# Accumulating transfers of a column pair's eight blocks into the HBM copy of x, written one per following row pair, in a two-layer retention and latent-attention trunk

## The chip, the cores and the metric

The kernel runs on one core of a Trainium2 chip. The metric is the device time of one execution in microseconds. Before the change three executions took 2494.59, 2503.17 and 2501.63 us; the median is 2501.63 us. One further execution was recorded by the profiler.

## The reference

The program is a trunk of two layers over 256 tokens (two row tiles of 128) with a residual stream `x` of width 2048, all in float32. Layer 0 is a RetNet retention layer with eight heads and a squared-ReLU MLP; layer 1 is a multi-head latent attention layer (MLA) with sixteen heads and the same MLP. What the change touches is how `x` takes in the result of a block:

```python
x = x + retention(h, ret_w_in[layer], ret_w_out[layer], ret_cos, ret_sin)
...
x = x + sq_relu_mlp(rms_norm(x, norm_mlp[layer]), mlp_w1[layer], mlp_w2[layer])

def sq_relu_mlp(h, w1, w2):
    return jnp.square(jax.nn.relu(h @ w1)) @ w2
```

`w1` is 2048 x 8192 and `w2` 8192 x 2048, so nearly all the work is matrix products whose weights come from HBM once.

## The kernel before, in words

**Products.** A float32 operand is split into a high part (a cast on ScalarE, line 183) and a low part (a subtraction on VectorE, line 184), and each product is made of three matmuls (lines 359 to 361). `quad` (line 285) works on one chunk of weights: 1 MB, 128 x 2048 numbers, loaded by the SP queue (line 288) into one of three `raw` buffers. A chunk holds a pair of weight rows (256 rows) for a pair of 512-wide output columns, as four 512-wide blocks. It is multiplied either plainly, with eight products (24 matmuls), or in a seven-product form after Winograd (21 matmuls), which needs extra sums of the weights on VectorE (lines 318 to 323). This document calls the work of one chunk a row, or row pair.

**Column pairs.** `gemm_pair` (line 336) runs 8 rows (4 groups of 2048 hidden columns give the MLP's second product 8 rows each) into PSUM blocks c11, c12, c21, c22, p1, p5, p6 and p7. `kinds` says which rows have seven products; for the first column pair of an MLP group these are rows 3, 5 and 7. `pair_out` (line 371) then copies c22, c12, c11, c21, p1 and p5 to SBUF on ScalarE (line 376) and makes `v` and `u` on VectorE (378, 379); `rest` (line 381), put one row later, changes `v` and `p5` (382, 383) and calls `done`. The result of a column pair is eight 128 x 512 blocks (256 KB each): for each of two columns and two row tiles two parts which have to be added, (c11, p1), (c12, v), (c21, u) and (c22, p5).

**Where the parts go.** The MLP's hidden columns are done in four groups, each as two column pairs of the first product (tensors `u...`) and two of the second (tensors `d...`). After the last group the parts are added to `x` in SBUF (`into_x`, line 150). After the first three groups, and after the first half of the retention heads (tensors `ro...`), they are added to a copy of `x` in HBM, `x_home` (eight tiles of 128 x 512, named `xh`), by transfers from GpSimd's queue that accumulate: `to_home`, lines 143 to 148. That makes 6 column pairs in each MLP and 2 in the retention layer, 14 in all, with 8 transfers each. `x_tiles` (line 131) brings `x` back from `x_home` ahead of its next use, also on GpSimd's queue (line 138).

**What sets the order.** While the program is written out, `later(n, fn)` (line 97) keeps a function for `n` rows; `tick` (line 105), at the end of each row, calls those that are due. So `later` decides at which place between the rows an instruction is written. The framework's planner then lays out one queue for each engine from the dependencies between instructions; the place where an instruction was written is its rank among those that are ready, and need not be its place in the queue. On the chip each engine works through its queue in order, and an instruction waits only for the semaphores of what it depends on. The tiles that hold the eight blocks come from one pool of 14 buffers (`f2k`, line 72).

Of the kernel before, what the change touches and what calls it, by code (L numbers as in the profile page):

```python
# [16 lines left out]
ALU = mybir.AluOpType  # L17
# [19 lines left out]
NT = 2  # L37
# [29 lines left out]
def yoco(ctx: ExitStack, tc: tile.TileContext, a):  # L67
    nc = tc.nc
# [28 lines left out]
    def later(n, fn):  # L97
        queue.append((clock[0] + n, next(count), fn))
# [29 lines left out]
    x_home = [[dram.tile([P, 512], F32, name=f"xh_{t}_{b}") for b in range(NB)] for t in range(NT)]  # L128
# [13 lines left out]

    def to_home(c, p):

        for j in range(2):
            for t in range(NT):
                for part in c[t][j]:
                    nc.gpsimd.dma_start(x_home[t][2 * p + j], part, accum_op=ALU.add)  # L148

    def into_x(done, c, p):  # L150
        for j in range(2):
# [572 lines left out]
    def ret_out_half(i):  # L724

        w = a["ret_w_out"]
        if i:
            x_tiles("ro")
        for p in range(2):
            first = LATE if i else HEAD  # L730

            def done(c, p=p):
                into_x(into_n1, c, p) if i else to_home(c, p)

            gemm_pair(w, p * 16 + 8 * i, halves[i], [k in first for k in range(8)], f"ro{i}{p}", done)
# [43 lines left out]
    def mlp(layer, act, r, done):  # L779
        w1, w2 = a[f"mlp_w1_{layer}"], a[f"mlp_w2_{layer}"]  # L780
        f0 = 0
        for gi, nf in enumerate(GROUPS):
# [34 lines left out]
            for p in range(2):  # L817
                if last and p and layer:
                    for b in (2, 3):
                        need(hid, 2 * nf)  # L820
                        gemm(
                            a[f"mlp_w2t_{layer}"], (b - 2) * nf, hid, 4 * nf, 512, f"d{layer}_{gi}{b}",
                            lambda acc, b=b: done(b, acc),
                        )
                    continue

                def add(c, p=p, last=last):
                    into_x(done, c, p) if last else to_home(c, p)

                kinds = [i in ((LATE if last else ODD) if p else SEVEN) for i in range(2 * nf)]  # L830
                gemm_pair(w2, p * 32 + 2 * f0, blocks, kinds, f"d{layer}_{gi}{p}", add)
# [359 lines left out]
```

## Time and profile before

| | |
|---|---|
| median of three executions | 2501.63 us (2494.59 to 2503.17) |
| the profiled execution | 2504.95 us |
| its span, first to last instruction | 2503.2 us |
| instructions | 31661 |
| VectorE busy | 2199.6 us (88%) |
| ScalarE busy | 1647.8 us (66%) |
| GpSimd busy | 252.0 us (10%) |
| moved by the DMA engines | 521.04 MB, 208 GB/s in the mean |
| mean granted TensorE clock | 0.997 |

Times are microseconds from the span's start. PE is the matmul part of TensorE, PEld its weight loads, DVE VectorE, ACT ScalarE, POOL GpSimd, SP the engine that issues the weight loads; a name with a q behind it is the engine's queue. The profile has the busy time of each engine, the span in slices, the DMA queues, the chain of work that ended last, the costliest groups of instructions and the DMA issues. In a group or a timeline, `out<-in` are the program's tensors without their numbers, so `d_c` is any of c11, c12, c21 and c22 of the MLP's second product, and the bracket at the end is the idle time of the engine before it and what ended it. Busy times of PE are modelled, since matmuls are pipelined.

### The profile page before, as it was taken

How to read it: one execution, taken by the hardware profiler on the slowest of the kernel's cores; microseconds unless marked ns; L12 is line 12 of the kernel's file. 1: busy time of each engine (PE TensorE's matmuls, PEld its weight loads, DVE VectorE, ACT ScalarE, POOL GpSimd, SP SyncE). 2: the span in 40 equal slices, each digit the busy share in tenths (PEclk: the TensorE clock that was granted, in tenths of full speed). 3: DMA queues.
4: the chain of work that ended last, by engine and by line, in shares of the span. 5: the costliest groups of instructions: out<-in, count | busy, mean ns of one | idle time of the engine just before them, and what ended most of it. 6: DMA issues, size and time to landing. Idle time of an engine off the chain costs nothing.

```text
span 2503.2 us, 31661 instructions
## 1 busy us (share of the span) xinstructions
PE 2458.7 (98%) x11614; PEld 2065.5 (83%) x11614; DVE 2199.6 (88%) x2892; ACT 1647.8 (66%) x2297; POOL 252.0 (10%) x308
## 2 busy tenths in 40 slices
PE   9999999999999999999999999999999999999999
PEld 7788887888888878878878888998888788787887
DVE  6799999889898989989989988776999899899896
ACT  6566666556667757667666777666677567676673
POOL 7300011000010110110110101110000101101100
PEclk9999999999999999999999999999999999999999
DMA  8555577555565785775865555444556856857764
GB/s 310 193 200 187 195 216 233 193 195 200 208 231 188 212 244 190 229 220 201 243 245 202 193 202 175 162 146 175 182 206 205 248 197 210 243 196 231 242 214 167
DMA packets 93403, 521.04 MB, mean 208 GB/s; under 512 B 11072, under 2 KB 12224, under 8 KB 40000
## 3 DMA queue, kind: packets, MB, share of 16 engines
q1 hardware_dynamic: 71856, 472.83, 53.3%
q0 software_dynamic: 21248, 46.15, 9.4%
q8 instruction: 91, 1.49, 0.2%
q14 instruction: 64, 0.52, 0.1%
q10 hardware_dynamic: 144, 0.05, 0.0%
HBM read 479.14 MB, written 39.85 MB: 207 GB/s over the span
## 4 chain that ended last, share of the span: by engine, by line
PE 76%; DVE 12%; DMA 7%; issue 2%; ACT 2%; POOL 1%; DVEq 0%; SPq 0%; ACTq 0%; POOLq 0%
PE u_c L360 6%; PE u_c L361 6%; PE u_c L359 6%; PE d_c L360 4%; PE d_c L361 4%; PE d_c L359 4%; DMA d_raw<-in_mlp_w 3%; DVE d_wl L184 3%; DMA u_raw<-in_mlp_w 3%; PE rp_c L360 2%; PE rp_c L359 2%; PE rp_c L361 2%; PE rq_acc L271 2%; PE rk_acc L271 2%; DVE u_wl L184 2%
## 5 line engine op out<-in xcount | busy, mean ns | idle before, releaser
L184 DVE TENSOR_TENSOR d_wl<-d_raw,d_wh 128x1024 fp32r<-128x1024 f32 (+1 forms) x256 | 279.0, 1115 | 27.8 <-ACT d_wh L183 27.7
L183 ACT CAST d_wh<-d_raw 128x1024 fp32r<-128x1024 f32 (+1 forms) x256 | 241.7, 974 | 87.3 <-PE d_c L361 43.5
L184 DVE TENSOR_TENSOR u_wl<-u_raw,u_wh 128x1024 fp32r<-128x1024 f32 (+1 forms) x256 | 277.4, 1110 | 16.7 <-ACT u_wh L183 16.7
L360 PE MATMUL u_c<-u_wl,n 128*128 128x512 f32 x712 | 280.0, 393 | 11.7 <-DVE u_wl L184 11.7
L183 ACT CAST u_wh<-u_raw 128x1024 fp32r<-128x1024 f32 (+1 forms) x256 | 240.9, 972 | 75.0 <-PE u_c L361 49.8
L359 PE MATMUL u_c<-u_wh,n 128*128 128x512 f32 x712 | 280.4, 395 | 0.0
L361 PE MATMUL u_c<-u_wh,n 128*128 128x512 f32 x712 | 279.1, 392 | 0.0
L360 PE MATMUL d_c<-d_wl,hid 128*128 128x512 f32 x660 | 258.1, 391 | 7.8 <-DVE d_wl L184 7.8
L359 PE MATMUL d_c<-d_wh,hid 128*128 128x512 f32 x660 | 259.1, 393 | 0.0
L361 PE MATMUL d_c<-d_wh,hid 128*128 128x512 f32 x660 | 257.6, 390 | 0.0
L183 ACT CAST u_wh<-u_u 128x1024 fp32r<-128x1024 f32 x104 | 107.8, 1054 | 115.2 <-PE u_c L361 59.2
L183 ACT CAST d_wh<-d_u 128x1024 fp32r<-128x1024 f32 x100 | 103.6, 1055 | 101.0 <-DVE d_u L323 57.5
L360 PEld LDWEIGHTS u_c<-u_wl,n 128*128 128x128 f32 x712 | 134.9, 189 | 42.4 <-DVE u_wl L184 15.1
L361 PEld LDWEIGHTS u_c<-u_wh,n 128*128 128x128 f32 x712 | 134.9, 189 | 28.2
L359 PEld LDWEIGHTS u_c<-u_wh,n 128*128 128x128 f32 x712 | 134.8, 189 | 27.4
L360 PEld LDWEIGHTS d_c<-d_wl,hid 128*128 128x128 f32 x660 | 124.3, 188 | 35.3 <-DVE d_wl L184 10.0
L183 ACT CAST rp_wh<-rp_raw 128x1024 fp32r<-128x1024 f32 x112 | 104.1, 945 | 69.2 <-PE rp_c L361 42.1
L361 PEld LDWEIGHTS d_c<-d_wh,hid 128*128 128x128 f32 x660 | 124.3, 188 | 25.8
L359 PEld LDWEIGHTS d_c<-d_wh,hid 128*128 128x128 f32 x660 | 124.3, 188 | 25.3
L184 DVE TENSOR_TENSOR u_wl<-u_u,u_wh 128x1024 fp32r<-128x1024 f32 x104 | 124.2, 1220 | 9.8 <-ACT u_wh L183 9.8
L148 POOL DMA_DIRECT2D xh<-d_c x48 | 41.9, 949 | 848.0 <-ACT d_c L376 847.6
L184 DVE TENSOR_TENSOR rp_wl<-rp_raw,rp_wh 128x1024 fp32r<-128x1024 f32 x112 | 118.9, 1090 | 3.8 <-ACT rp_wh L183 3.2
(567 smaller groups left out, 6684.7 us busy)
## 6 DMA issues: line engine op xcount, KB each, us to landing
u_raw<-in_mlp_w SPq DMA_DIRECT2D x128, 1024.0 KB, 5.4
d_raw<-in_mlp_w SPq DMA_DIRECT2D x120, 1024.0 KB, 4.9
rp_raw<-in_ret_w_gv SPq DMA_DIRECT2D x56, 1024.0 KB, 4.9
ro_raw<-in_ret_w_out SPq DMA_DIRECT2D x32, 1024.0 KB, 4.9
uq_raw<-in_mla_w_uq SPq DMA_DIRECT2D x24, 768.0 KB, 4.3
rq_raw<-in_ret_w_qk SPq DMA_DIRECT2D x16, 1024.0 KB, 5.2
rk_raw<-in_ret_w_qk SPq DMA_DIRECT2D x16, 1024.0 KB, 4.9
xh<-d_c POOLq DMA_DIRECT2D x48, 256.0 KB, 5.6
```

The source lines that it names most:

```text
L148: nc.gpsimd.dma_start(x_home[t][2 * p + j], part, accum_op=ALU.add)
L183: nc.scalar.copy(h, src)
L184: return nc.vector.tensor_tensor(l, src, h.bitcast(F32), op=ALU.subtract)
L271: nc.tensor.matmul(acc[f], wh[:, cols], a.rearrange("p i s -> p (i s)"), start=k == 0, stop=k == nk - 1)
L359: nc.tensor.matmul(dst, ah, bh, start=n == 0, stop=False)
L360: nc.tensor.matmul(dst, ah, bl, start=False, stop=False)
L361: nc.tensor.matmul(dst, al, bh, start=False, stop=n == total[key] - 1)
```

## The change

`to_home` no longer writes its eight transfers in one place. They are put in the order first parts (c11, c21, c12, c22), second parts (p1, u, v, p5), and the n-th is given to `later(n, ...)`, so it is written n rows after `rest`. Before, the written order was c11, p1, c21, u, c12, v, c22, p5, all at the place of `rest`. Nothing else differs.

```diff
     def to_home(c, p):
 
-        for j in range(2):
-            for t in range(NT):
-                for part in c[t][j]:
-                    nc.gpsimd.dma_start(x_home[t][2 * p + j], part, accum_op=ALU.add)
+        def send(t, j, i):
+            nc.gpsimd.dma_start(x_home[t][2 * p + j], c[t][j][i], accum_op=ALU.add)
+
+        for n, (i, j, t) in enumerate(itertools.product(range(2), range(2), range(NT))):
+            later(n, lambda i=i, j=j, t=t: send(t, j, i))
```

## The prediction

> **What bounds the kernel now.** First the page's span and busy times, then the view of the waits of PE, then the table of windows.
>
> ```profile
> span 2503.2 us, 31661 instructions
> PE 2458.7 (98%) x11614; PEld 2065.5 (83%) x11614; DVE 2199.6 (88%) x2892; ACT 1647.8 (66%) x2297; POOL 252.0 (10%) x308
> ```
> ```profile
> PE u_c L360 <- DVE u_wl L184: 11.7, 6, 3.1
> PE d_c L360 <- DVE d_wl L184: 7.8, 5, 2.4
> PE ro_c L360 <- DVE ro_wl L184: 1.6, 1, 1.6
> ```
> ```profile
> 790.00:830.00 40.00, 40.00 (x186) 33.28 (x186) 37.65 (x47) 29.34 (x40) 0.00 (x0) 1.00 0.59 203
> 850.00:890.00 40.00, 38.51 (x171) 31.55 (x170) 35.55 (x38) 25.39 (x30) 7.08 (x8) 1.00 0.91 261
> 895.00:935.00 40.00, 38.18 (x169) 31.29 (x168) 35.08 (x38) 23.97 (x30) 6.98 (x8) 1.00 0.84 242
> 935.00:975.00 40.00, 40.00 (x186) 33.31 (x185) 37.22 (x48) 30.00 (x40) 0.00 (x0) 1.00 0.57 203
> ```
>
> The matmuls fill the span: 2458.7 of 2503.2 us leave 44.5 us. In the table each row is a window of 40 us; behind its length stand the busy times of PE, PEld, DVE, ACT and POOL with their counts, then the granted clock, the share of the DMA engines and GB/s. Without transfers into x_home (POOL 0.00) PE is busy for 40.00 of 40.00 us with the DMA engines at 0.57 to 0.59. The two windows with POOL at about 7 us are those in which eight transfers each go into x_home: the DMA engines are at 0.91 and 0.84, and PE lacks 1.5 and 1.8 us. The waits of PE (total, times, longest) show the same over the whole span: 11.7 + 7.8 + 1.6 = 21.1 us in 12 waits in the products that run beside such transfers, all for a low part of the weights from VectorE. In the timeline each stands in the rows behind one of the 14 column pairs that go to x_home. So 21.1 us, 0.84% of 2503.2, is all that these transfers cost PE.
>
> How a transfer does this is seen in the column pair that ends at 853 us. The Pool timeline, then VectorE's, the merged chain, PE's timeline, and the page's row of these loads with their median time to landing:
>
> ```profile
> 853.68 0.94 POOL L148 DMA_DIRECT2D xh<-d_c  x1 [110.61 <-ACT d_c L376]
> 856.40 0.88 POOL L148 DMA_DIRECT2D xh<-d_c  x1 [1.78 <-ACT d_c L376]
> 857.82 1.76 POOL L148 DMA_DIRECT2D xh<-d_c  x2 [0.54 <-ACT d_c L376]
> 866.35 0.86 POOL L148 DMA_DIRECT2D xh<-d_p  x1 [6.77 <-DMA xh<-d_c]
> 867.98 0.86 POOL L148 DMA_DIRECT2D xh<-d_u  x1 [0.77 <-DVE d_u L318]
> 868.52 1.21 POOL L148 DMA_DIRECT2D xh<-d_v  x1
> 869.06 1.56 POOL L148 DMA_DIRECT2D xh<-d_p  x1
> 896.26 0.86 POOL L148 DMA_DIRECT2D xh<-d_c  x1 [25.64 <-ACT d_c L376]
> ```
> ```profile
> 877.85 1.22 DVE L318 TENSOR_TENSOR d_u<-d_raw 128x1024 f32<-128x1024 f32 x1 [3.50 <-DMA d_raw<-in_mlp_w]
> ```
> ```profile
> 869.04 8.71 DMA d_raw<-in_mlp_w
> ```
> ```profile
> 880.99 0.50 PE L360 MATMUL d_c<-d_wl,hid 128*128 128x512 f32 x1 [1.49 <-DVE d_wl L184]
> ```
> ```profile
> d_raw<-in_mlp_w SPq DMA_DIRECT2D x120, 1024.0 KB, 4.9
> ```
>
> Four transfers go out between 853.68 and 858.7, four more between 866.35 and 869.06. A weight load issued at 869.04, on top of the second four, takes 8.71 us where the median is 4.9, VectorE idles for 3.50 us before line 318, and PE stands for 1.49 us at 880.99 (part of the 7.8 above). So the aim of the change is real: spread out, these eight would meet fewer loads.
>
> **The change part by part.** *Removed and added:* nothing. 14 pairs x 8 = 112 transfers before and after, same sizes, the same three kinds of waits (for the copy or VectorE's sum that makes the part; for the first part into the same block to have landed). Their issues cost Pool the same, at 0.9 to 1.2 us each:
>
> ```profile
> L148 POOL DMA_DIRECT2D xh<-d_c x48 | 41.9, 949 | 848.0 <-ACT d_c L376 847.6
> ```
>
> *Moved:* 112 instructions are written later, by 0 to 7 rows. The question on which everything hangs is whether an instruction that is written later is issued later. Two facts decide, and both can be read in before.
>
> First, nothing holds Pool back. It has between the transfers of one pair no other instruction (the seven rows above follow each other, and the next is the next pair's at 896.26), and it is idle for 848.0 us ahead of the d_c group, 847.6 of it until ScalarE has copied the block. A written place between rows 3 and 4 is no semaphore: it ties Pool to no row. A transfer goes out when its part exists and the first part has landed.
>
> Second, the queue does not keep the written order even where there is another instruction to be passed. Three rows of ScalarE's timeline, one of VectorE's, two of Pool's around the start of the output projection:
>
> ```profile
> 852.79 0.59 ACT L376 COPY d_c<-d_c 128x512 f32<-128x512 f32 x1 [0.26 <-PE d_c L361]
> ...
> 855.51 0.59 ACT L376 COPY d_c<-d_c 128x512 f32<-128x512 f32 x1 [0.26 <-PE d_c L361]
> ...
> 856.95 1.07 ACT L376 COPY d_c<-d_c 128x512 f32<-128x512 f32 x2
> ```
> ```profile
> 862.65 0.68 DVE L383 TENSOR_TENSOR d_p<-d_p,d_u 128x512 f32<-128x512 f32 x1
> ```
> ```profile
> 1683.19 1.18 POOL L138 DMA_DIRECT2D x_wo<-xh  x2
> 1700.92 2.60 POOL L173 TENSOR_TENSOR qn_r<-qn_m,neg_half 128x8 f32<-128x8 f32 x1 [16.56 <-DVE qn_m L172]
> ```
>
> The first block copied, at 852.79, is c22: rows 3, 5 and 7 of this pair have seven products, c22 gets its last product inside row 6, and the others end in row 7. Its transfer is the first on Pool (853.68), though it is the seventh of eight in the written order, and all eight are written behind `rest`, whose last sum runs at 862.65. So a transfer written 9 us later goes first, because its data is there. The last two rows say the same from further off: the loads of x_wo are written after the last query block's norm (the last of the eight qn_r), and two of them are in the queue ahead of it, by 17.7 us. The planner places by readiness; the written place is only a rank between instructions that are ready at once.
>
> So what does the new rank change? The order on Pool is now, by the causes in the brackets, c22, c12, c11, c21, then p1, u, v, p5. Before, the written order has p1 ahead of c21, c12 and c22, u ahead of c12 and c22, v ahead of c22; after, it does not. Each of these flips is between a first part, out by 858.7, and a second part that has to wait for a landing until 866 or so: never both ready. Within the first four (c11, c21, c12, c22) and within the second four (p1, u, v, p5) the rank is the same in both versions. So the queue comes out as it was: **0 us** on the path, 0 on Pool, 0 on SP.
>
> No other engine's queue has an instruction moved. The buffers (14 in the pool) come free when a transfer has read its part, thus when they did; the loads of x back from x_home stand behind the same landings.
>
> *The unknown, from both sides.* No row shows such a transfer held back by its written place, so the cost of that is bounded: below by -21.1 us, when all 12 waits of PE go; above by the order rival below, +24 us. I take 0, since the nearest rows, those of Pool, show the queue filled by readiness.
>
> A price for the spreading, if it happened, comes from the DMA queues of two windows of 35 us, 780 to 815 and 850 to 885:
>
> ```profile
> q1 hardware_dynamic: 1008, 7.34, 60.8%
> ```
> ```profile
> q1 hardware_dynamic: 913, 6.69, 52.3%
> q0 software_dynamic: 1152, 2.10, 39.8%
> ```
>
> Without transfers a 1.05 MB weight load takes 0.608 x 35 / 7.0 = 3.04 us of all 16 engines; a transfer takes 0.398 x 35 / 8 = 1.74 us. A row lasts about 42.58 / 8 = 5.3 us (853.68 to 896.26), stalls included. One load and one transfer per row make 4.78 us, 90% of a row: it fits, with little to spare.
>
> The Trainium skill, in "DMA: Bandwidth & Descriptors", section "Anatomy of one DMA — SWDGE (gpsimd) path", gives about 2.0 us plus bytes / 436e3 for a DMA from GpSimd's queue: by that a 256 KB transfer would take the engines an estimated 0.6 us, eight of them 4.8 us, and bunched transfers would hardly delay a load. The 39.8% measured here, three times as much, speaks against it for accumulating ones; by the page's price spreading would bring next to nothing even if it happened.
>
> *Sum:* 2504.95 + 0 for the profiled execution (span 2503.2 and 1.7 us around it). That execution lies 3.3 us above the median of the three others, 2501.63, which I take for the prediction: **2501.6 us**.
>
> **The rivals.** *Forecast: the written place does not reach the queue.* That is also the case in which the change doesn't do what it says. 2501.6 us; the three executions of before span 8.6 us, so a median within 0.3% (7.5 us, about what a measurement of this kernel can tell from no change) is likely: 2494 to 2509. Chance 0.75, with 0.71 inside the 0.3% and 0.02 outside on each side.
>
> *The transfers are spread, one per row.* For it speaks only that the planner could keep the rank of instructions in some way that these rows don't show; against it the two facts above. With 90% of the DMA engines' time used in those rows, I estimate three quarters of the stalls as gone: 21.1 x 0.75 = 16 us, 2501.6 - 16 = 2486 us; 2480.5 if all go, 2491 with half. Chance 0.15, faster.
>
> *The written order rules on Pool within a pair, and it is slower.* Now c11 and c21 stand ahead of c12 and c22. If the queue followed that, c22's transfer, ready at 853.4, would wait for c11's copy at 857.8, 4 us later, and four would go out in 4 x 0.87 = 3.5 us and not in 5. One transfer more, 1.74 us, then stands in the way of the load issued in that time: up to 14 x 1.74 = 24 us, 2526; half of it, where there is slack, 2514. It decides from the point at which c22 is no longer first on Pool. Against it: under the old written order c22 was seventh and went first. Chance 0.06.
>
> *Buffers:* transfers that go later hold their tiles longer, and a copy at line 376 could wait for one of the 14. At the next pair's copies seven of the eight old ones would be out, so 9 are needed of 14: no wait. Where the second pair of a group is followed by the hidden blocks of the next product, which take 6 more, a wait for one landing (8.0 us at the median) less a row, 2.7 us, in 6 places gives 16 us; it needs the spreading first and would eat its gain: 2502. Chance 0.04.
>
> ```profile
> DMA to landing us min/median/max: 4.0/8.0/13.8
> ```
>
> **How the numbers follow.** Faster by over 0.3%: 0.15 + 0.02 = 0.17. Slower by over 0.3%: 0.06 + 0.02 = 0.08, and 0.01 from the buffers, 0.09. Within: 0.74. The range reaches from 2484, which takes in the likeliest time of the spread case, to 2511, a little above the upper end of the forecast's own 2494 to 2509, since the slower order starts there. Left out are the better end of the spreading and the worse half of the order rival, under 2 in 10.
>
> **What would show it.** Right: in Pool's timeline the eight transfers of a pair still go out as four within some 5 us and four within 3, in the order d_c x4, d_p, d_u, d_v, d_p, the first of them ahead of the other copies; in the waits of PE about 12 waits for a low part in `u_c`, `d_c` and `ro_c`, some 21 us; the DMA share in those windows at 0.84 to 0.91. Wrong, faster: transfers some 5 us apart over 35 us, waits of PE gone, loads near their 4.9 us. Wrong, slower: d_c transfers all behind the last copy, or new waits of ScalarE at line 376 for a transfer. What would make the prediction wrong altogether is a planner for which a later rank moves an instruction on an idle queue, or reshuffles queues that have none of these instructions.

## The result, and the profile after

The changed kernel takes 2502.07 us at the median (2495.93 to 2507.79, 12 executions), the kernel before 2500.97 us beside it (2493.05 to 2507.13, 12 executions). The ratio is 1.0004, with a 95% interval of 0.9989 to 1.002: no difference that can be measured. The profiled execution of the changed kernel took 2506.1 us.

The page's span and busy times, the waits of PE for a low part (total, times, longest) and two windows, as shown of before:

```profile
span 2504.3 us, 31661 instructions
PE 2463.4 (98%) x11614; PEld 2069.5 (83%) x11614; DVE 2199.7 (88%) x2892; ACT 1648.3 (66%) x2297; POOL 251.6 (10%) x308
```
```profile
PE u_c L361 <- DVE u_wl L185: 11.1, 8, 2.2
PE d_c L361 <- DVE d_wl L185: 6.5, 4, 2.5
...
PE ro_c L361 <- DVE ro_wl L185: 0.3, 1, 0.3
```
```profile
850.00:890.00 40.00, 39.81 (x176) 32.64 (x175) 37.06 (x41) 25.26 (x31) 7.08 (x8) 1.00 0.89 257
895.00:935.00 40.00, 38.12 (x162) 31.04 (x161) 35.18 (x38) 23.94 (x28) 6.17 (x8) 0.96 0.80 224
```

As many instructions, much the same waits (17.9 us in 13, before 21.1 in 12), the DMA engines about as busy where the transfers go out (0.89 and 0.80, before 0.91 and 0.84). Pool's timeline around the same column pair:

```profile
852.92 0.94 POOL L146 DMA_DIRECT2D xh<-d_c  x1 [110.61 <-ACT d_c L377]
855.65 0.88 POOL L146 DMA_DIRECT2D xh<-d_c  x1 [1.79 <-ACT d_c L377]
857.06 1.76 POOL L146 DMA_DIRECT2D xh<-d_c  x2 [0.54 <-ACT d_c L377]
865.44 0.86 POOL L146 DMA_DIRECT2D xh<-d_p  x1 [6.62 <-ACT d_wh L184]
868.38 0.86 POOL L146 DMA_DIRECT2D xh<-d_u  x1 [2.07 <-DVE d_u L319]
868.92 1.22 POOL L146 DMA_DIRECT2D xh<-d_v  x1
869.46 1.57 POOL L146 DMA_DIRECT2D xh<-d_p  x1
894.19 0.86 POOL L146 DMA_DIRECT2D xh<-d_c  x1 [23.17 <-ACT d_c L377]
```

Four go out within 5 us and four within 4, in the order of before, although they are now written over eight rows. The causes named in the brackets at d_p and d_u (a cast, a weight sum) are only what ended on another engine at that moment; as in before, a second part waits for the first one to land. The two programs that the framework makes of the two sources are equal as well, instruction by instruction with their operands, buffer addresses, semaphores and awaited values: the queues of Pool (423 entries), ScalarE (3279), TensorE (11649), VectorE (3570) and SP (979) are the same. Only the numbers in the names of temporaries and the line numbers differ. The chip ran the same program twice. So what differs between the two profiles (PE lacks 0.2 us in the first window, and 1.5 in before) is what two executions of one program differ by, and a single stall is to be read with care.

### The profile page after: what moved, and what is told of

Its sections match the earlier page's. It is cut to its first block, busy times and chain, and to the rows that moved or that the text cites. A ratio compares the mean times of both kernels' runs of the same rounds, so it can differ in the third digit from the quotient of the medians.

```text
span 2504.3 us, 31661 instructions
## 1 busy us (share of the span) xinstructions
PE 2463.4 (98%) x11614; PEld 2069.5 (83%) x11614; DVE 2199.7 (88%) x2892; ACT 1648.3 (66%) x2297; POOL 251.6 (10%) x308
## 3 DMA queue, kind: packets, MB, share of 16 engines
q8 instruction: 91, 1.49, 0.2%
## 4 chain that ended last, share of the span: by engine, by line
PE 79%; DVE 10%; DMA 6%; ACT 2%; issue 2%; POOL 1%; DVEq 0%; ACTq 0%; POOLq 0%
PE u_c L361 6%; PE u_c L362 6%; PE u_c L360 6%; PE d_c L361 5%; PE d_c L362 5%; PE d_c L360 5%; DMA u_raw<-in_mlp_w 4%; PE rp_c L360 2%; PE rp_c L362 2%; PE rp_c L361 2%; PE rq_acc L272 2%; PE rk_acc L272 2%; DMA d_raw<-in_mlp_w 2%; DVE d_wl L185 2%; PE ro_c L361 1%
## 5 line engine op out<-in xcount | busy, mean ns | idle before, releaser
L185 DVE TENSOR_TENSOR d_wl<-d_u,d_wh 128x1024 fp32r<-128x1024 f32 x100 | 119.0, 1218 | 5.0 <-ACT d_wh L184 5.0
```

The source lines that it names most:

```text
L185: return nc.vector.tensor_tensor(l, src, h.bitcast(F32), op=ALU.subtract)
```

## The experiments

Two questions are left. What do these transfers cost at all, and would spreading them have paid, if the change had done it? Six of the experiments edit the kernel before (e1, e3, e7, e8, e10, e12), the others the changed kernel, which is the same program. The times are medians; the ratios are to the kernel before, measured beside each, with 95% intervals.

**What the transfers cost.** They are left out.

```diff
     def to_home(c, p):
+        return
```

> Leaves out all 112 accumulating transfers, so that the output lacks the sums of three MLP groups in each layer and of half the retention heads. Theory (the 21.1 us of PE waits behind the column pairs are the whole cost of these transfers): about 2480 us, ratio 0.9915, and no waits of PE for a low part in the d, u and ro products. Rival (those waits come from the copies and sums at a pair's end, which stay here): 2495 to 2501 us, ratio 0.998 to 1.000, with 10 us or more of the waits left.

Measured: 2473.87 us, ratio 0.9899 (0.9881 to 0.9916). The page's busy times and the first window:

```profile
PE 2448.8 (99%) x11614; PEld 2061.8 (83%) x11614; DVE 2198.4 (89%) x2892; ACT 1649.6 (67%) x2297; POOL 154.7 (6%) x196
```
```profile
850.00:890.00 40.00, 40.00 (x178) 33.13 (x177) 38.26 (x43) 26.13 (x31) 0.00 (x0) 1.00 0.60 211
```

The transfers cost 26.6 us (2500.45 beside it, less 2473.87), not the 21.1 us of the waits. The rest stands in the busy time of PE, which falls with the same 11614 matmuls from 2458.7 to 2448.8 us. Profiled execution against profiled execution the two terms close: before, 21.1 us of waits and 9.9 us of busy time make 31.0, and 2504.95 - 2473.71 is 31.2. The changed kernel has 17.9 + 14.6 = 32.5, and 2506.1 - 2473.71 is 32.4. So the transfers cost 1.5 times (before) and 1.8 times (changed) the waits that they cause. e1 lies below the 2480 us of its theory for this reason.

**What makes a transfer dear.** The transfers write their block instead of adding it.

```diff
-                    nc.gpsimd.dma_start(x_home[t][2 * p + j], part, accum_op=ALU.add)
+                    nc.gpsimd.dma_start(x_home[t][2 * p + j], part)
```

> The kernel before with plain writes into the copy of x in place of accumulating ones, so the output keeps only the last part written into each block; number, size, order and waits of the transfers are the same. If it is the accumulation (a read and a write of HBM, and 1.74 us of all 16 DMA engines for 256 KB) that makes a bunch late: the software queue's share in a pair's window falls from 39.8% to under 20%, and most of the 26.6 us go, 2476 to 2484 us. Rival (any eight transfers of 256 KB in a bunch cost it): 2494 to 2509 us, share of the queue above 30%.

Measured: 2478.84 us, ratio 0.9914 (0.9891 to 0.9936). The DMA queues in the window 850 to 885 (packets, MB, share of 16 engines):

```profile
q1 hardware_dynamic: 1119, 8.16, 66.7%
q0 software_dynamic: 640, 2.10, 15.3%
```

The same 2.10 MB take 15.3% instead of 39.8% of 35 us: 0.67 us of all 16 engines per transfer instead of 1.74, with the transfers still in two bunches. It is the accumulation that makes the bunches hurt, but perhaps not by this price alone: the first parts land sooner, so the second bunch starts at 861.88 us and not at 866.35, and meets other loads. The run doesn't separate the two. The estimate of 0.6 us that the prediction worked out from the Trainium skill, "DMA: Bandwidth & Descriptors", section "Anatomy of one DMA — SWDGE (gpsimd) path", agrees with these plain writes, and with the accumulating ones it doesn't.

**Whether the written order matters on Pool.** The first parts are chained in the written order by a dependency.

```diff
+        sent = []
+        for i, j, t in itertools.product(range(2), range(2), range(NT)):
+            sent.append(nc.gpsimd.dma_start(x_home[t][2 * p + j], c[t][j][i], accum_op=ALU.add))
+            if i == 0 and len(sent) > 1:
+                queued_behind(sent[-1], sent[-2])
```

> The kernel before with one thing forced: the first parts of a pair stand on Pool's queue as c11, c21, c12, c22, so c22 no longer goes first. My theory (the order of the four does not matter, they are four transfers beside the same loads): 2494 to 2509 us, ratio 0.997 to 1.003. The order rival: 2514 us, at most 2526, ratio 1.005 to 1.010.

Measured: 2499.89 us, ratio 0.9997 (0.9985 to 1.001). Pool's timeline has the four in one go, none ahead of the copy of c11, the third of the four copies:

```profile
858.63 3.64 POOL L147 DMA_DIRECT2D xh<-d_c  x4 [114.77 <-ACT d_c L377]
865.00 0.86 POOL L147 DMA_DIRECT2D xh<-d_p  x1 [2.73 <-issue]
```

Even where the order does reach the queue, it costs nothing that can be measured.

**Spreading with a wait that reaches the queue.** Each transfer depends on the last low part that VectorE has made in the row at which it is written, so that Pool waits for a semaphore (against the changed kernel; `...` marks code left out):

```diff
+    last_low = [None]
...
         def send(t, j, i):
-            nc.gpsimd.dma_start(x_home[t][2 * p + j], c[t][j][i], accum_op=ALU.add)
+            ins = nc.gpsimd.dma_start(x_home[t][2 * p + j], c[t][j][i], accum_op=ALU.add)
+            tc.add_manual_dep(
+                ins.ins, last_low[0].ins.name,
+                mybir.DependencyInfo(mybir.DependencyClass.Sync, mybir.DependencyReason.DATA), reason="row",
+            )
...
             low = split(wh[:, : n * 512], wl[:, : n * 512], src)
+            last_low[0] = low
```

> The changed kernel with a real wait added: each transfer waits for the last low part that VectorE makes in its row, so eight transfers of a pair go out one per row. Spread case: the transfers stand about 5 us apart over some 37 us and three quarters of the waits of PE go: 2486 us, ratio 0.994; 2480.5 if all go. Rival (buffers held longer, a copy at a pair's end or a hidden block waits for one): 2498 to 2502 us, ratio 0.999 to 1.000, with waits of ScalarE or VectorE for a transfer. Rival (with 90% of the DMA engines' time used, loads are late anyway): waits of PE keep 15 us or more, 2495 to 2501 us.

Measured: 2482.88 us, ratio 0.9932 (0.9916 to 0.9948). Pool's timeline (the first two and the last of the pair's eight) and the waits of PE:

```profile
858.67 0.94 POOL L147 DMA_DIRECT2D xh<-d_c  x1 [116.07 <-ACT d_p L383]
865.44 0.88 POOL L147 DMA_DIRECT2D xh<-d_c  x1 [5.83 <-DVE d_wl L190]
...
895.50 0.86 POOL L147 DMA_DIRECT2D xh<-d_p  x1 [3.76 <-DVE d_wl L190]
```
```profile
PE d_c L367 <- DVE d_wl L190: 4.4, 4, 1.7
...
PE u_c L367 <- DVE u_wl L190: 1.2, 3, 0.8
```

Now they are one per row, and 17.6 us are gained. Nine of 26.6 us stay: by its profile 5.6 us of waits, and 3.7 us more of PE's busy time than in e1 (2452.5 on its page). Neither ScalarE nor VectorE waits for a transfer.

**Other spacings.** The next three are shown against e2. Two per row, all else as in e2:

```diff
-            later(n, lambda i=i, j=j, t=t: send(t, j, i))
+            later(n // 2, lambda i=i, j=j, t=t: send(t, j, i))
```

> As e2_spread, but two transfers of a pair per row, so eight in four rows. If the cost is the bunching (one load and one transfer fill a row's DMA time to 90%, one load and two to about 123%): loads fall behind for four rows and the gain is between the kernel before and one per row, 2488 to 2496 us, ratio 0.995 to 0.998. Rival (it is the wait itself that helps, by taking the transfers away from the pair's end): as e2_spread, 2483 us, ratio 0.993.

Measured: 2497.88 us, 0.9976 (0.9959 to 0.9994), a little above both expectations. One per row again, but released by the row's first low part instead of its last:

```diff
-            last_low[0] = low
+            if part == 0:
+                last_low[0] = low
```

> As e2_spread, one per row, but each transfer waits for the first low part of its row and not for the last, so it does not start when the buffer of the weights comes free and the next load starts. If the rest of the cost (2482.9 - 2473.9 = 9 us) comes from transfer and load starting together: 2476 to 2480 us, ratio 0.991 to 0.9925. Rival (the rest is the DMA engines being 90% full, wherever in the row the transfer stands): 2481 to 2485 us.

Measured: 2495.6 us, 0.9979 (0.9961 to 0.9997), far above both. Pool's timeline shows that the spacing did not stay the same, as the expectation had taken for granted: in these two rows one gap is 7.33 us and the next 2.01.

```profile
880.38 0.86 POOL L147 DMA_DIRECT2D xh<-d_p  x1 [7.33 <-DVE d_wl L190]
883.25 0.86 POOL L147 DMA_DIRECT2D xh<-d_u  x1 [2.01 <-DVE d_wl L190]
```

Two per row, and one per row at another moment, lose most of the gain of e2. Eight transfers over eight rows cost 9 us over the time without any in e2 and, by the ratios, some 20 in e6, so the number per row isn't the whole answer. All eight held until the fourth row behind the pair, together:

```diff
-            later(n, lambda i=i, j=j, t=t: send(t, j, i))
+            later(3, lambda i=i, j=j, t=t: send(t, j, i))
```

> All eight transfers of a pair wait for the low part that VectorE makes three rows after the sums at the pair's end: a real wait, but the same bunches, later. If only the spacing matters and not the place: as before, 2494 to 2509 us, ratio 0.997 to 1.003, waits of PE again 15 to 27 us, three rows later. If any later place helps (the loads that a pair's end makes late are then past): 2486 to 2492 us. If bunching got worse because the first four now go out at once: 2510 us or more.

Measured: 2504.09 us, 1.0017 (1.0003 to 1.0032). The waits of PE:

```profile
PE u_c L367 <- DVE u_wl L190: 16.1, 11, 2.6
PE d_c L367 <- DVE d_wl L190: 4.4, 6, 1.1
```

The first goes out at 874.43 us in Pool's timeline, 21 us later than before, and the eight cost about what they cost before: being late is no gain by itself.

**Only the second parts moved.** The first four go out at the pair's end as before; the second four wait for rows 5 to 8, one in each (e9), or for row 5 all together (e11). e9 against e2:

```diff
-            tc.add_manual_dep(
+            if i:
+                tc.add_manual_dep(
```

> As e2_spread, but only the second parts (p1, u, v, p5) wait for their rows, the fifth to the eighth after the pair; the first four go out at once as in the kernel before. If the three weight buffers cover one bunch of four and the cost comes from the second bunch on top of the first: as e2_spread, 2481 to 2486 us, ratio 0.992 to 0.994. Rival (each bunch costs its half): about 2491 us, ratio 0.996.

Measured: 2476.01 us (2473.31 to 2477.54), ratio 0.9897 (0.9877 to 0.9917): the time without any transfers, within the spread. It lies below both expectations, and is the fastest version that still does all the work. The page's busy times, Pool's timeline and the first window:

```profile
PE 2448.4 (99%) x11614; PEld 2061.6 (83%) x11614; DVE 2199.7 (89%) x2892; ACT 1648.4 (67%) x2297; POOL 254.2 (10%) x308
```
```profile
852.34 0.94 POOL L147 DMA_DIRECT2D xh<-d_c  x1 [110.61 <-ACT d_c L384]
855.06 0.88 POOL L147 DMA_DIRECT2D xh<-d_c  x1 [1.78 <-ACT d_c L384]
856.48 1.76 POOL L147 DMA_DIRECT2D xh<-d_c  x2 [0.54 <-ACT d_c L384]
877.43 0.86 POOL L147 DMA_DIRECT2D xh<-d_p  x1 [19.19 <-DVE d_wl L191]
883.34 0.86 POOL L147 DMA_DIRECT2D xh<-d_u  x1 [5.05 <-DVE d_wl L191]
887.48 0.86 POOL L147 DMA_DIRECT2D xh<-d_v  x1 [3.27 <-DVE d_wl L191]
...
893.67 1.22 POOL L147 DMA_DIRECT2D xh<-d_p  x1
```
```profile
850.00:890.00 40.00, 40.00 (x178) 33.11 (x177) 38.25 (x42) 25.96 (x30) 6.17 (x7) 1.00 0.84 247
```

PE is busy for 40.00 of 40.00 us with the DMA engines at 0.84, as busy as in the window 895 to 935 of before, which lost 1.8 us. Then the second four as one bunch, against e9:

```diff
-            later(n, lambda i=i, j=j, t=t: send(t, j, i))
+            later(4 * i, lambda i=i, j=j, t=t: send(t, j, i))
```

> As e9_half, but the second parts of a pair all wait for the same row, the fifth after the pair: two bunches of four, some 20 us apart instead of about 8. If the three weight buffers take up one bunch and what costs is that the second comes before the loads have caught up: as e9_half, 2474 to 2480 us, ratio 0.989 to 0.992. Rival (what helps is one transfer per row, any bunch of four in the middle of a pair costs): 2485 to 2495 us, ratio 0.994 to 0.998.

Measured: 2478.45 us, 0.9901 (0.9884 to 0.9917). Even as one bunch they cost little at this place (Pool's timeline, the first of the four; the last begins at 883.28):

```profile
881.66 0.86 POOL L147 DMA_DIRECT2D xh<-d_p  x1 [19.82 <-DVE d_wl L191]
```

**Two bunches too close, or the place?** From these runs I had formed a theory: the loads bear one bunch, and a second one within some 13 us is too much. A rival fits as well: it matters which load the transfers meet. e12 sends only one bunch, the second parts, at the place that the second bunch has in the kernel before. The first parts are left out. `send` has the dependency of e2:

```diff
+        for j, t in itertools.product(range(2), range(NT)):
+            later(1, lambda j=j, t=t: send(t, j, 1))
```

> The first parts' transfers are left out (so that half of what belongs into x_home never gets there); the four second parts go out together, tied to the last low part of the second row behind rest, at about 865 us in the pair looked at, which is where the second bunch of the kernel before goes. By the theory of two bunches too close (the loads can bear one bunch of four, and a second one within some 13 us of it is what makes VectorE late) nothing stalls: about 2475 us, the time without transfers, and no wait of PE for a low part of u, d or ro. By the rival (the place: transfers in these rows hit loads with no slack left, while those at the pair's end and from row 5 on are hidden) most of the waits stay: 2490 us or more and at least 10 us of such waits. In between, 2480 to 2487 us, both count.

Measured: 2493.16 us, ratio 0.997 (0.9954 to 0.9985). Pool's timeline, the waits of PE, the step of the chain that is the load, VectorE's row and PE's row:

```profile
864.94 0.94 POOL L147 DMA_DIRECT2D xh<-d_p  x1 [122.84 <-DVE d_wl L190]
...
866.66 1.91 POOL L147 DMA_DIRECT2D xh<-d_p  x1
```
```profile
PE u_c L367 <- DVE u_wl L190: 7.9, 8, 2.5
PE d_c L367 <- DVE d_wl L190: 4.5, 5, 1.7
```
```profile
868.07 8.56 DMA d_raw<-in_mlp_w
```
```profile
877.07 1.23 DVE L325 TENSOR_TENSOR d_u<-d_raw 128x1024 f32<-128x1024 f32 x1 [3.69 <-DMA d_raw<-in_mlp_w]
```
```profile
880.21 0.50 PE L367 MATMUL d_c<-d_wl,hid 128*128 128x512 f32 x1 [1.69 <-DVE d_wl L190]
```

My theory falls. A single bunch of four, with no other before it, costs some 18 us over the time without transfers (a ratio of 0.997 against 0.9899) when it goes out at 865 us, and 12.4 us of waits are there; a bunch of four at 882 us (e11, 0.9901) costs next to nothing, with another at the pair's end besides.

Which load it meets can be read in the kernel without transfers. SP's timeline has loads in couples, at 857.76 and 861.88, 868.16 and 871.22, 877.63 and 879.97; by the times from issue to landing (5.0 and 4.7 us) the first loads of the first two couples are there at 862.8 and 872.9. The first load of each couple is that of a seven-product row, whose weight sums VectorE makes:

```profile
865.78 1.22 DVE L315 TENSOR_TENSOR d_u<-d_raw 128x1024 f32<-128x1024 f32 x1
...
873.39 1.22 DVE L315 TENSOR_TENSOR d_u<-d_raw 128x1024 f32<-128x1024 f32 x1
```

The first is taken up 3.0 us after it landed, since VectorE is still busy with the pair's own sums; the second 0.5 us after. In e9 the load at 857.30 meets the first bunch and takes 7.6 us, and VectorE doesn't wait for it; the next of this kind, at 867.70, meets nothing and takes 4.9. In e12 that second load, at 868.07, takes 8.56 us, VectorE waits 3.69 and PE 1.69. Two other kernels with transfers in these rows, e2 and then e6, give the same relation in VectorE's and PE's timelines:

```profile
876.67 1.22 DVE L325 TENSOR_TENSOR d_u<-d_raw 128x1024 f32<-128x1024 f32 x1 [2.79 <-DMA d_raw<-in_mlp_w]
```
```profile
879.81 0.50 PE L367 MATMUL d_c<-d_wl,hid 128*128 128x512 f32 x1 [0.78 <-DVE d_wl L190]
```
```profile
877.00 1.23 DVE L326 TENSOR_TENSOR d_u<-d_raw 128x1024 f32<-128x1024 f32 x1 [2.24 <-DMA d_raw<-in_mlp_w]
```
```profile
880.14 0.50 PE L368 MATMUL d_c<-d_wl,hid 128*128 128x512 f32 x1 [0.23 <-DVE d_wl L190]
```

VectorE's wait less PE's is 2.0 us in e12, e2 and e6, and in before (3.50 and 1.49). So this load, the tight one, bears some 2.5 us of delay, 0.5 ahead of VectorE and 2.0 between VectorE and PE, and the first one some 5. The 2.0 us are one allowance for both: in the profile of the changed kernel VectorE waits 0.99 us for the first load and 1.11 for the second, and PE 0.19.

That the place decides is shown by e12 beside e11. The slack is much the same in the other MLP pairs of the kernel without transfers: the load that SP issues some 16 us behind the pair's first copy is taken up 0.1 to 0.5 us after it landed in all 12, the one some 6 us behind it 2.2 to 3.4 us after in 11 of them, and the loads of rows with eight products lie for 5 to 9 us before their first use. Later loads of seven-product rows are taken up within 1.2 us too; the bunch of e11 goes out just behind the start of such a load (881.40 us, 5.7 us to landing) and slows the one after it (8.6 us), which is that of a plain row. In e12, 11 of the 13 waits of PE stand at the same distance, 12 to 15 us behind the last of its transfers.

Why e6 is so much worse than e2 stays partly open: in the pair looked at, the u load at 891.20 took 8.2 us in e6 and the one at 890.60 took 6.9 in e2, and PE waited 1.79 and 0.24 us; that the moment of release decides which load is met was not tried by itself.

**Fewer transfers.** GpSimd adds the two parts, so that four transfers go out instead of eight (e7), or four one every second row (e8).

```diff
+        for t, j in ((0, 0), (1, 0), (0, 1), (1, 1)):
+            a0, a1 = c[t][j]
+            nc.gpsimd.tensor_tensor(a0, a0, a1, op=ALU.add)
+            nc.gpsimd.dma_start(x_home[t][2 * p + j], a0, accum_op=ALU.add)
```

> No spreading; GpSimd adds the two parts of a block in SBUF first (four additions of 128x512 a pair), and four transfers a pair go out instead of eight. If the cost goes with the bytes in a bunch: half of the 26.6 us that e1_none shows, or less, since a bunch of four is shorter: 2480 to 2488 us, ratio 0.992 to 0.995. Rival (GpSimd's additions slow VectorE down, which is busy in 89% of these rows): 2495 us or more, with VectorE's instructions in these windows longer than before.

> GpSimd's sums as in e7_sums, and the four transfers wait for the last low part of every second row. If bytes and spacing are both the cost: near the kernel without transfers, 2475 to 2480 us, ratio 0.990 to 0.992, with at most 3 us of waits of PE for low parts. Rival as for e7_sums (additions slow VectorE): 2485 us or more.

The diff is e7's. Measured: e7 2520.97 us, 1.0078 (1.0047 to 1.011); e8, with e2's dependency and `later(2 * n, ...)`, 2513.86 us, 1.0047 (1.003 to 1.0063). Pool's and VectorE's timelines of e7:

```profile
866.60 1.85 POOL L147 TENSOR_TENSOR d_c<-d_c,d_u 128x512 f32<-128x512 f32 x1
```
```profile
867.21 1.79 DVE L382 TENSOR_TENSOR d_v<-d_p,d_v 128x512 f32<-128x512 f32 x1
...
869.53 2.00 DVE L383 TENSOR_TENSOR d_p<-d_p,d_u 128x512 f32<-128x512 f32 x1
```

VectorE's sums, 0.68 us in the kernel before (its line 383, shown in the prediction), take 1.8 to 2.0 us beside GpSimd's, and VectorE is busy for 2250.9 us instead of 2199.6. These are rows in which VectorE is the engine that is late, and the kernel loses more than it gains by four transfers fewer. In e7 these also go out beside the tight load (865.94 to 874.11 us; the load at 869.63 takes 7.9 us); in e8 that load takes 5.3, and the kernel is still slower than before. The Trainium skill has a cause in "SBUF — State Buffer", section "Who interferes with whom": VectorE and GpSimd share one pair of ports under an exclusive lock; these rows agree.

## Why the prediction was right, point by point

- **The written place does not reach the queue: 0 us.** Right, and shown twice: by Pool's timeline and by queues that are equal entry for entry. Its first fact (nothing in Pool's queue ties a transfer to a row) and its second (the planner places by readiness) agree with this; the second was inferred from the queues, and no run tested it by itself. That 2501.6 us came within 0.5 us is in part luck: it was a median of three executions of a kernel whose executions spread over 14 us.
- **The order within the two fours doesn't change, and no other queue is touched.** Right: c22 still goes first, and the buffer addresses are the same.
- **"So 21.1 us ... is all that these transfers cost PE."** Too small. Without them 26.6 us are gained at the median, and 31.2 between the profiled executions; the missing term, 10 us, is the busy time of PE. The lower bound of -21.1 us for the unknown was too small for the same reason.
- **The price of spreading, 2486 us, and its bounds 2480.5 and 2491.** 2482.88 with a real wait, inside them. The best that these transfers allow, 2476.01, lies below the lower bound, since that counted the waits alone.
- **"Spread out, these eight would meet fewer loads."** The wrong reason. By SP's timeline 7 of the 10 weight loads from 857 to 903 us take over 6.4 us in e9, and 6 of the 10 from 858 to 906 in before; but in the pair looked at, the load that is taken up 0.5 us after landing is none of e9's slow ones (4.9 us). e12 delays that load and the next, and stalls.
- **The price of a transfer, 1.74 us of all engines.** e10 agrees: at 0.67 us two bunches of eight transfers cost 5 us instead of 26.6, though the second also goes out sooner.
- **The order rival, 2514.** Falls: forced to happen (e3), it gives 0.9997. Its term, one transfer more in the way of the load, supposed that this load has no slack; the first four meet the loads right behind the pair, which by the kernel without transfers have some.
- **The buffers rival, 2502.** Not seen where transfers are really late (e2).

## What to carry to other kernels

Writing an instruction later does not delay it, where its queue is idle and a planner fills the queues by readiness: a pace needs a dependency, and the first look is at the queues, whether they differ at all. Before spreading transfers out, leave them out, to know what they cost, and read for each load in their way how long after landing it is taken up: bunches beside loads with slack cost nothing that can be measured here, and a single one beside the tight load some 18 of 26.6 us. Here one dependency on the second parts, away from that load, brought 1.0%.

## What the runs showed of the hardware

After a short stall of PE the granted clock can fall. Two windows of 10 us, with and behind a stall of 1.88 us in the changed kernel, and the row of the stall:

```profile
920.00:930.00 10.00, 8.12 (x30) 6.52 (x30) 8.96 (x10) 3.35 (x4) 0.00 (x0) 0.83 0.58 213
930.00:940.00 10.00, 10.00 (x46) 8.29 (x45) 7.50 (x8) 6.19 (x8) 0.00 (x0) 1.00 0.57 213
```
```profile
921.90 0.51 PE L361 MATMUL u_c<-u_wl,n 128*128 128x512 f32 x1 [1.88 <-DVE u_wl L185]
```

The granted clock falls to 0.83 in the 10 us with the stall, and is back at 1.00 in the next. In the kernel before, which is the same program, a stall of 1.82 us at the same place leaves it at 1.00 (the window 895 to 935 of the prediction). So it happens with some stalls and not with others. It explains only a part of PE's longer busy time. Added up in windows of 10 us, with the span's start and end left out, the clock falls short of full speed by 8.5 us in before, 13.6 in the changed kernel, 3.4 in e12 and 1.7 in e1. So, as an estimate, it makes up 6.8 of the 9.9 us by which PE is busy longer than in e1, 11.9 of 14.6 in the changed kernel, and 1.7 of 6.1 in e12 (2454.9 us busy). What makes up the rest is open. The spread of the executions shrinks with the stalls as well: 2494.04 to 2510.36 us for the kernel before (11 executions), 2473.31 to 2477.54 for e9 beside it (6).

An accumulating transfer of 256 KB takes 2.6 times as much of the DMA engines' time as a plain write of the same block (1.74 and 0.67 us, before and e10, window 850 to 885).
